# Four wide Strassen groups for the merge gates, and projections by tokens, in a hybrid encoder block

## The chip, the cores and the metric

The kernel runs on one core of one Trainium2 chip. The metric is device microseconds from the start to the end of one launch, as the median of three runs. TensorE (PE) multiplies, VectorE (DVE), ScalarE (ACT) and GpSimd (POOL) work on rows, and SyncE (SP) issues the transfers.

## The reference

One layer of a hybrid encoder, 512 tokens by 2048, in float32. A normed input is projected to 10752 columns; two attention branches, each gated by a SiLU, are projected to 2048 columns, merged by sigmoid gates, projected once more and added to the input:

```python
h = rmsnorm(x, norm_g[l])
proj = jnp.einsum('bsd,dc->bsc', h, w_in[l])
qa, ka, va, za, qb, kb, vb, zb, ga, gb = jnp.split(proj, SPLIT_POINTS, axis=-1)
...
ya = jnp.einsum('bsc,cd->bsd', oa * jax.nn.silu(za), w_out_a[l])
qb = axial_rope(rmsnorm(qb.reshape(B, S, N_HEADS_B, DH_B), q_norm_g[l]))
kb = axial_rope(rmsnorm(kb.reshape(B, S, N_KV_B, DH_B), k_norm_g[l]))
...
yb = jnp.einsum('bsc,cd->bsd', ob * jax.nn.silu(zb), w_out_b[l])
merged = jax.nn.sigmoid(ga) * ya + jax.nn.sigmoid(gb) * yb
x = x + jnp.einsum('bsd,de->bse', merged, w_o[l])
return rmsnorm(x, final_g)
```

Branch A is a differential attention of 8 heads, branch B a grouped one of 8 query and 2 key heads.

## The kernel before

Every product is made of three matmuls: both operands are split into a high part and a low rest (`hi_lo`: the high part is cast by ACT on line 111, the rest subtracted by VectorE on line 112), and high by high, low by high and high by low are summed in PSUM. The weights stream from memory into eight raw tiles; `split_w` takes three pairs of split tiles in turn, so the casts run up to three tiles ahead of TensorE.

The stages in order of time: the norm of x and a first group of plain columns (to 69.5 us); a narrow Strassen group (to 109.8); two wide Strassen groups for the other columns of q, k and v (`strassen_wide`, 111.3 to 263.7); twelve narrow Strassen groups by columns for the gates (`strassen`, 265.5 to 750.4), four for the SiLU gates z and then eight for the merge gates; the attention (750.4 to 1109.8), whose heads are interleaved with plain blocks of q and k and then with the projection `w_out_b` as filler (`fill`); the projection `w_out_a` with the merge (1109.8 to 1196.8); four narrow Strassen groups for `w_o` with the residual and the last norm.

A narrow group multiplies 512 tokens by 512 columns in seven products (a11, a12, s1, s2, s3, s4, a22) of 48 matmuls, 256 columns wide, on line 241: 336 matmuls. A wide group covers 512 tokens by 1024 columns with the same seven products of 48 matmuls, 512 wide, on line 322. A product of a narrow gate group takes two weight tiles of 128x1024, each cast once; VectorE also subtracts weight tiles (line 216) and adds products (line 642), and ACT applies the gate's function (line 643).

The order on each engine is that in which the code is recorded, moved by a scheduler's priorities; each engine then runs in order, and so does SP, whose transfers all pass through one queue. A waiting instruction keeps everything behind it on its engine waiting.

After each of the first ten gate groups `rope_b(n)` turns one head of branch B (n below 8 are query heads, 8 and 9 key heads): SP loads it (`cols`, line 595), ACT squares its four token blocks (line 600), GpSimd makes the reciprocal root (`rb`, lines 107 and 108), VectorE does two half-width multiplications, one full multiplication and an addition (lines 611 to 613), ACT scales key heads by `rb` (line 616), and SP stores it (line 617). The order of heads is `to_rope`. The attention's first heads load what was stored (line 673).

PSUM is eight banks. `new_banks` opens a pool of single banks or of pairs of banks; `share_banks` names the rings for accumulators (`acc`) and for the rest (`aux`), and `bank` takes the next of a ring. In the attention there are two `acc` and six `aux` banks. A head's `scores(i)` (branch A, lines 788 and 789) make four tiles of weights, `turn_p` transposes them on TensorE (line 732), `finish` multiplies with the values, and `norm` (branch A, lines 813 to 824) sums squares by two matmuls and applies the norm through ACT (816, 817, 820) and VectorE (from 821).

Of the kernel before, what the change touches and what calls it, by code (L numbers as in the profile page):

```python
# [17 lines left out]
P = 128  # L18
D = 2048
# [32 lines left out]
def hybrid_block_kernel(  # L52
# [16 lines left out]
    def new_banks(unit):  # L69
        ps_pools.close()  # L70
        banks["pool"] = unit, ps_pools.enter_context(
            tc.tile_pool(name="ps_" + unit, bufs=1, space=bass.MemoryType.PSUM))
# [120 lines left out]
    def strassen(w, c_left, c_right, act, natural, tmp, done, tail=None, before={}):  # L193
# [24 lines left out]
        def product(name, b, by_row=False, parts=None):  # L218
            if name in before:
                before[name]()  # L220
            ps = [acc_tile(256) for _ in range(2)] if by_row else acc_tile(2, 256)
# [5 lines left out]
            for n, (p, u) in enumerate(steps):  # L227
                if p not in parts:
                    parts[p] = split_w(b[p])
                hi, lo = parts[p]  # L230
# [138 lines left out]
    gg = dram.tile([2 * D, S], F32, name="gg")  # L369
    og = dram.tile([2 * BW, S], F32, name="og")  # L370
    yg = dram.tile([D, S], F32, name="yg")
# [59 lines left out]
    with tc.tile_pool(name="xs", bufs=1) as xs:  # L431
# [119 lines left out]
        with tc.tile_pool(name="wide", bufs=1) as wide:  # L551
            for n, blocks in enumerate(WIDE_BLOCKS):
                def kept(th, ch, v, blocks=blocks):
                    keep_cols(blocks[ch * 4:ch * 4 + 4], th * 2, 2, v)

                strassen_wide(w_in, column_pieces(blocks[:4]), column_pieces(blocks[4:]), xq, wide, kept, late=n == 0)
        slots[:] = slots[0:2] + slots[4:6] + slots[2:4] + slots[6:8]

        with tc.tile_pool(name="sp", bufs=6) as sp:
# [29 lines left out]
            def rope_b(n):  # L589
# [31 lines left out]
            to_rope = [0, 8, 1, 2, 3, 4, 5, 9, 6, 7]  # L621
# [15 lines left out]
            for c0, n, func, dst in ((O_ZA, BW, AF.Silu, zg[0:BW]), (O_ZB, BW, AF.Silu, zg[BW:]),  # L637
                                     (O_GA, D, AF.Sigmoid, gg[0:D]), (O_GB, D, AF.Sigmoid, gg[D:])):
                for g in range(0, n, S):
                    def gate(th, ch, ps, sb, g=g, func=func, dst=dst):  # L640
                        v = tmp()
                        nc.vector.tensor_tensor(out=v, in0=ps, in1=sb, op=ALU.add)
                        nc.scalar.activation(out=v, in_=v, func=func)
# [6 lines left out]
                    if to_rope:  # L650
                        rope_b(to_rope.pop(0))

    share_banks(acc=[4, 5], aux=[6, 7, 0, 1, 2, 3])
# [66 lines left out]
    class Head:  # L720
# [6 lines left out]
        def turn_p(self):  # L727
            self.pt = []
            for j in range(NT):
# [151 lines left out]
    def og_act(k):  # L881
        return tuple(v[:, k % 8, :] for v in ogq[k // 8])
# [24 lines left out]
    def fillers():  # L907
# [9 lines left out]
        for n in range(8):  # L917
            def yb_done(c, ps, n=n):
                j = c * 8 + n
                g = load_rows(gg, NK + j, "kq", 2)  # L920
                nc.vector.tensor_tensor(out=g, in0=ps, in1=g, op=ALU.mult)
                nc.sync.dma_start(out=yg[j * P:(j + 1) * P, :], in_=g)

            steps = stream_steps(w_out_b, [(n * P, P), (1024 + n * P, P)], 8, False, lambda k: og_act(8 + k), yb_done)
            for last in (12, 12, 16, 16):
# [15 lines left out]
    with tc.manual_schedule(engines={mybir.EngineType.PE}):  # L941
# [7 lines left out]
        for n, head in enumerate(heads):  # L949
            f = [int(c) for c in FILLS[n]]  # L950
            last = heads[n - 1] if n else None
            if n + 1 < len(heads):
                heads[n + 1].double()
            head.scores(0)
# [4 lines left out]
            head.scores(2)  # L959
            head.scores(3)  # L960
# [18 lines left out]
    share_banks(acc=list(banks["aux"] + banks["acc"]), aux=[])  # L979
# [7 lines left out]
    with tc.tile_pool(name="ya", bufs=1) as yp:  # L987
        def row(src, j, tag):
            g = yp.tile([P, S], F32, name="rows", tag=tag, bufs=2)
            nc.sync.dma_start(out=g, in_=src[j * P:(j + 1) * P, :])  # L990
            return g

        for n in range(4):
            mg = yp.tile([P, 4, S], F32, name="mg", tag="mg")

            def ya_done(c, ps, n=n, mg=mg):
                j = c // 2 * 8 + n * 2 + c % 2
                g = row(gg, j, "g")
                yb = row(yg, j, "yb")

                with tc.high_priority() if n == 3 else ExitStack():
                    nc.vector.tensor_tensor(out=g, in0=ps, in1=g, op=ALU.mult)
                    nc.vector.tensor_tensor(out=mg[:, c, :], in0=g, in1=yb, op=ALU.add)

            stream(w_out_a, [(n * 256, 256), (1024 + n * 256, 256)], 8, False, og_act, ya_done)
            b = slice(n * 2, n * 2 + 2)
            a11, a12, a21, a22 = (mg[:, k * 2:k * 2 + 2, t * 256:t * 256 + 256]
                                  for t, k in ((0, 0), (0, 1), (1, 0), (1, 1)))
# [3 lines left out]
            m_sums = {"a11": (a11, ()), "a12": (a12, ()), "s1": (s, (s, a21, a22, ALU.add)),  # L1012
                      "s2": (s, (s, s, a11, ALU.subtract)), "s3": (s3, (s3, a11, a21, ALU.subtract)),
                      "s4": (s, (s, a12, s, ALU.subtract)), "a22": (a22, ())}

            def put(name, b=b, m_sums=m_sums):
                src, first = m_sums[name]
# [188 lines left out]
```

## Time and profile before

| | us |
|---|---|
| median of three runs (lowest, highest) | 1368.19 (1367.49, 1370.12) |
| the profiled execution's own time | 1369.72 |
| its span | 1367.5 |
| TensorE busy in the span | 1337.8 |
| VectorE / ACT / GpSimd busy | 1086.4 / 709.5 / 166.9 |

The span is the time from the first to the last instruction of the profiled execution; the own time counts what lies around it too. An engine's busy time is an average over stages with different limits, so the stages are to be read one by one. A matmul's listed duration contains its pipeline, so the pace of matmuls is read from start to start. "Idle before" names what ended a wait.

### The profile page before, as it was taken

The page shows a single profiled execution, that of the slowest core. Times are in us where ns is not written, and L with a number is a line of the kernel's source. Part 1 is how long each engine was busy: PE and PEld are TensorE (multiplying, and loading weights), DVE is VectorE, ACT ScalarE, POOL GpSimd, SP SyncE. Part 2 cuts the span into 40 slices and gives each one's busy share as a digit, 9 for nine tenths or more (in the row PEclk, how much of TensorE's full clock was granted, in tenths as well). Part 3 has the DMA queues.
Part 4 walks back from the last instruction along what each step waited for, and adds up shares of the span by engine and source line. Part 5 has one row for each costly group of instructions (what it writes and reads, how often), then busy time and mean ns, then how long its engine had stood idle before and what let it go on. Part 6 is the DMA issues. An engine that isn't in the chain of part 4 may idle for free.

```text
span 1367.5 us, 22737 instructions
## 1 busy us (share of the span) xinstructions
PE 1337.8 (98%) x8905; PEld 1232.9 (90%) x8905; DVE 1086.4 (79%) x1339; ACT 709.5 (52%) x1119; POOL 166.9 (12%) x154
## 2 busy tenths in 40 slices
PE   6999999999999999999999999999899999999997
PEld 5998888899999999999999888888688888899997
DVE  5976977777888777888876487977899948799886
ACT  7643343344445444444444576666777743354444
POOL 1000000040000000000000411331321010004322
PEclk9999999999999999999999999999999999999999
DMA  8244663564444545444455684455665446473233
GB/s 292 78 140 138 188 197 95 171 197 147 131 139 126 161 154 162 128 136 130 126 154 169 209 247 120 143 155 156 198 187 158 147 147 213 141 252 118 93 94 124
DMA packets 198892, 214.11 MB, mean 157 GB/s; under 512 B 11760, under 2 KB 159488, under 8 KB 198144
## 3 DMA queue, kind: packets, MB, share of 16 engines
q1 hardware_dynamic: 198784, 212.65, 50.0%
q8 instruction: 70, 1.15, 0.4%
q14 instruction: 38, 0.31, 0.1%
HBM read 172.76 MB, written 35.65 MB: 152 GB/s over the span
## 4 chain that ended last, share of the span: by engine, by line
PE 88%; DVE 5%; ACT 2%; DMA 2%; issue 2%; SPq 1%; POOL 0%; DVEq 0%; POOLq 0%; ACTq 0%
PE acc L241 45%; PE acc L182 23%; PE acc L322 11%; PE aux L745 3%; DVE w_lo L112 2%; PE aux L732 2%; PE aux L858 1%; PE aux L788 1%; PE aux L789 1%; DVE w_raw L216 1%; DMA xt<-in_x_dram 1%; ACT w_hi L111 0%; PE aux L481 0%; DMA lam<-in_lambda_k_dram 0%; DMA rows<-og 0%
## 5 line engine op out<-in xcount | busy, mean ns | idle before, releaser
L111 ACT CAST w_hi<-w_raw 128x1024 fp32r<-128x1024 f32 x357 | 374.9, 1051 | 495.7 <-PE acc L241 308.2
L112 DVE TENSOR_TENSOR w_lo<-w_raw,w_hi 128x1024 fp32r<-128x1024 f32 x357 | 449.1, 1260 | 159.3 <-ACT w_hi L111 158.9
L216 DVE TENSOR_TENSOR w_raw<-w_raw 128x1024 f32<-128x1024 f32 x136 | 170.8, 1256 | 2.1
L241 PE MATMUL acc<-a2h,w_hi 128*128 128x256 f32 x384 | 108.7, 283 | 0.0
L241 PE MATMUL acc<-a2l,w_hi 128*128 128x256 f32 x384 | 108.7, 283 | 0.0
L241 PE MATMUL acc<-a2h,w_lo 128*128 128x256 f32 x384 | 108.7, 283 | 0.0
L241 PEld LDWEIGHTS acc<-a2h,w_hi 128*128 128x128 f32 x384 | 73.7, 192 | 0.0
L241 PEld LDWEIGHTS acc<-a2l,w_hi 128*128 128x128 f32 x384 | 73.7, 192 | 0.0
L241 PEld LDWEIGHTS acc<-a2h,w_lo 128*128 128x128 f32 x384 | 73.7, 192 | 0.0
L700 DVE TENSOR_REDUCE nmax<-aux 128x1 f32<-128x512 f32 x96 | 61.4, 679 | 3.0 <-PE aux L789 3.0
L182 PE MATMUL acc<-a1h,w_hi 128*128 128x512 f32 (+1 forms) x160 | 57.3, 363 | 0.2 <-ACT a1h L485 0.2
L182 PE MATMUL acc<-a1h,w_lo 128*128 128x512 f32 (+1 forms) x160 | 56.5, 358 | 0.0
L182 PE MATMUL acc<-a1l,w_hi 128*128 128x512 f32 (+1 forms) x160 | 56.3, 357 | 0.1
L241 PE MATMUL acc<-a1h,w_hi 128*128 128x256 f32 x192 | 54.4, 283 | 1.6 <-DVE wide_u L330 1.6
L182 PE MATMUL acc<-a2h,w_hi 128*128 128x512 f32 (+1 forms) x160 | 55.6, 350 | 0.0
L182 PE MATMUL acc<-a2l,w_hi 128*128 128x512 f32 (+1 forms) x160 | 55.5, 348 | 0.0
L182 PE MATMUL acc<-a2h,w_lo 128*128 128x512 f32 (+1 forms) x160 | 55.4, 347 | 0.0
L241 PE MATMUL acc<-s2h,w_lo 128*128 128x256 f32 x192 | 54.5, 284 | 0.6 <-DVE w_lo L112 0.6
L241 PE MATMUL acc<-s1h,w_lo 128*128 128x256 f32 x192 | 54.3, 283 | 0.0
L241 PE MATMUL acc<-s3l,w_hi 128*128 128x256 f32 x192 | 54.3, 283 | 0.0
L241 PE MATMUL acc<-s3h,w_lo 128*128 128x256 f32 x192 | 54.3, 283 | 0.0
L241 PE MATMUL acc<-a1l,w_hi 128*128 128x256 f32 x192 | 54.3, 283 | 0.0
(353 smaller groups left out, 4177.6 us busy)
## 6 DMA issues: line engine op xcount, KB each, us to landing
w_raw<-in_w_in_dram SPq DMA_DIRECT2D x144, 512.0 KB, 3.8
w_raw<-in_w_in_dram SPq DMA_DIRECT2D x64, 256.0 KB, 4.1
w_raw<-in_w_o_dram SPq DMA_DIRECT2D x32, 512.0 KB, 4.2
cols<-pv SPq DMA_DIRECT2D x36, 256.0 KB, 3.3
gg<-kept SPq DMA_DIRECT2D x32, 256.0 KB, 2.4
w_raw<-in_w_out_b_dram SPq DMA_DIRECT2D x32, 256.0 KB, 3.7
rows<-gg SPq DMA_DIRECT2D x32, 256.0 KB, 3.4
w_raw<-in_w_out_a_dram SPq DMA_DIRECT2D x32, 256.0 KB, 3.2
```

Of the source, the lines that this page charges most:

```text
L111: nc.scalar.copy(out=hi, in_=src)
L112: nc.vector.tensor_tensor(out=lo, in0=src, in1=hi.bitcast(F32), op=ALU.subtract)
L182: nc.tensor.matmul(out=acc[b][:, place], lhsT=l, rhs=r, start=first and kc == order[0] and k == 0 and i == 0, stop=last and kc == order[-1 ...
L216: nc.vector.tensor_tensor(out=d, in0=u, in1=v, op=ALU.subtract)
L241: nc.tensor.matmul(out=ps[u] if by_row else ps[:, u, :], lhsT=l, rhs=r, start=n % (2 if by_row else 4) == 0 and k == 0 and i == 0, stop=n ...
L322: nc.tensor.matmul(out=ps[:, u, :], lhsT=l[:, kk, sl], rhs=r[:, k, :], start=kk == 0 and i == 0, stop=kk == H - 1 and i == 2)
L700: nc.vector.tensor_reduce(out=nmax, in_=sps, axis=AX.X, op=ALU.max, negate=True)
L732: nc.tensor.transpose(out=tp[:, i * P:(i + 1) * P], in_=self.p[i][:, j * P:(j + 1) * P], identity=ident)
L745: nc.tensor.matmul(out=o, lhsT=l, rhs=r, start=j == 0 and i == 0, stop=j == NT - 1 and i == 2)
L788: nc.tensor.matmul(out=sp, lhsT=qs[:, sl], rhs=kh, start=True, stop=False)
L789: nc.tensor.matmul(out=sp, lhsT=qs[:, sl], rhs=kl, start=False, stop=True)
L858: nc.tensor.matmul(out=sp, lhsT=l, rhs=r, start=n == 0, stop=n == 2)
```

## The change

Eight narrow merge-gate groups become four wide ones, which now stand right behind the two wide groups of q, k and v, ahead of the SiLU gates; their result `gg` is kept by tokens (512 by 4096) and not by columns. Both output projections are made by tokens (four accumulators of 128 tokens by 512 columns). The merged rows are then turned for `w_o` by 64 transposes on TensorE (`merged_turned`), the last lot of them inside the first product of the next stage, through the new argument `amid` of `strassen`.

Because the gate groups that are left are four, the ten heads of `rope_b` are handed out three, three, two and two behind them; their multiplications and additions are GpSimd's. `new_banks` claims all places of a pool in a fixed order. When the filler of `w_out_b` begins, two `aux` banks go over to the accumulators; heads that run with under six `aux` banks (`few`) share out their filler in another way and transpose in two parts. A head's norm moves behind the next head's `turn_p`. `w_o` has four accumulators and four other banks instead of eight accumulators.

```diff
     def new_banks(unit):
...
+        n = {"bank": 1, "pair": 2}[unit]
+        for i in range(8 // n):
+            pool.tile([P, n, S], F32, name="place", tag=f"{unit}{i}")
+        banks["pool"] = unit, pool
...
+            for g in range(0, 2 * D, 2 * S):
+                def merge_gate(th, ch, v, g=g):
+                    nc.scalar.activation(out=v, in_=v, func=AF.Sigmoid)
+                    c = g + ch * S
+                    nc.sync.dma_start(
+                        out=gg[th * 256:th * 256 + 256, c:c + S].rearrange("(u p) n -> p u n", p=P), in_=v)
+
+                strassen_wide(w_in, [(O_GA + g, S)], [(O_GA + g + S, S)], xq, wide, merge_gate)
...
-                    tc.keep_in_program_order(nc.vector.tensor_tensor(out=d, in0=s, in1=m, op=ALU.mult))
-                nc.vector.tensor_tensor(out=v, in0=v, in1=tcb, op=ALU.mult)
-                nc.vector.tensor_tensor(out=v, in0=v, in1=t2, op=ALU.add)
+                    nc.gpsimd.tensor_tensor(out=d, in0=s, in1=m, op=ALU.mult)
+                nc.gpsimd.tensor_tensor(out=v, in0=v, in1=tcb, op=ALU.mult)
+                nc.gpsimd.tensor_tensor(out=v, in0=v, in1=t2, op=ALU.add)
...
-            to_rope = [0, 8, 1, 2, 3, 4, 5, 9, 6, 7]
+            to_rope = [(0, 8, 1), (2, 3, 4), (5, 9), (6, 7)]
...
-            for c0, n, func, dst in ((O_ZA, BW, AF.Silu, zg[0:BW]), (O_ZB, BW, AF.Silu, zg[BW:]),
-                                     (O_GA, D, AF.Sigmoid, gg[0:D]), (O_GB, D, AF.Sigmoid, gg[D:])):
-                for g in range(0, n, S):
+            for c0, dst in ((O_ZA, zg[0:BW]), (O_ZB, zg[BW:])):
+                for g in range(0, BW, S):
...
-                    if to_rope:
-                        rope_b(to_rope.pop(0))
+                    for n in to_rope.pop(0):
+                        rope_b(n)
...
+        ring = banks["aux"]
+        banks["acc"] += [ring.pop(0), ring.pop(0)]
+        for n in range(4):
+            def yb_done(t, ps, n=n):
...
+            steps = stream_steps(w_out_b, [(n * S, S)], 8, True, lambda k, t: og_act(8 + k, t), yb_done)
...
+            few = len(banks["aux"]) < 6
...
-            fill(f[1] - 1)
+            fill(f[1] - few)
+            if few:
+                head.turn_p((0, 1))
+                fill(1)
+                head.turn_p((2, 3))
+            else:
+                head.turn_p()
             if last:
                 last.norm()
-            fill(1)
-            head.turn_p()
-            fill(f[2])
+            fill(f[2] - few)
...
-    share_banks(acc=list(banks["aux"] + banks["acc"]), aux=[])
+    share_banks(acc=banks["acc"], aux=banks["aux"])
...
+        def merged_turned(n, rows):
+
+            qs = [[aux(2, 256) for _ in range(2)] for _ in range(2)]
+            for th in range(2):
+                for kh in range(2):
+                    for j in range(2):
+                        for u in range(2):
+                            nc.tensor.transpose(out=qs[th][kh][:, j, u * P:u * P + P],
+                                                in_=rows[th * 2 + u][:, kh * 256 + j * P:kh * 256 + j * P + P],
+                                                identity=ident)
...
+            steps = stream_steps(w_out_a, [(n * 256, 256), (1024 + n * 256, 256)], 8, True, og_act, ya_done)
+            for i, _ in enumerate(steps):
+                if i == 2 and n:
+                    put = merged_turned(n - 1, turned_rows[-1])
...
+        strassen(w_o, 0, 256, mq, True, y_tmp, o_first, before={k: (lambda k=k: put_last(k)) for k in names[1:]},
+                 amid={"a11": lambda: put_last("a11")})
```

How the instructions stand now is shown at three places. On ACT, at the start of the second gate group, before the change (heads 8; the casts from `w_hi_3418` on are the group's fourth tile and later, `bsq` is a head's squares, `kept` a gate):

```order
L643 ACTIVATE kept_3291<-kept_3291 128x512
L600 ACTIVATE bsq_3297,rb_94<-cols_3295 128x128 x4
L111 CAST w_hi_3418<-w_raw_3320 128x1024
L111 CAST w_hi_3449<-w_raw_3314 128x1024
L616 ACTIVATE cols_3295<-cols_3295,rb_94 128x128 x4
L256 COPY kept_3387<-acc_3330 128x512
L111 CAST w_hi_3477<-w_raw_3316 128x1024
```

The same place after it, where the group begins with head 0 and then has head 8:

```order
L659 ACTIVATE kept_4975<-kept_4975 128x512
L617 ACTIVATE bsq_4981,rb_94<-cols_4979 128x128 x4
L115 CAST w_hi_5132<-w_raw_5034 128x1024
L617 ACTIVATE bsq_4996,rb_94<-cols_4994 128x128 x4
L115 CAST w_hi_5163<-w_raw_5028 128x1024
L633 ACTIVATE cols_4994<-cols_4994,rb_94 128x128 x4
L263 COPY kept_5101<-acc_5044 128x512
L115 CAST w_hi_5191<-w_raw_5030 128x1024
L617 ACTIVATE bsq_5015,rb_94<-cols_5013 128x128 x4
```

The scaling of head 8 (line 616, now 633) keeps its place ahead of the copy and of the cast of product s1's second tile, and a second head's squares have come between.

On SP, about the third gate group, before the change (one store and one load of a head in the group):

```order
L645 DMA zg_82<-kept_3694 128x2x256
L645 DMA zg_82<-kept_3755 128x2x256
L617 DMA pv_86<-cols_3759 128x512
L595 DMA cols_4679<-pv_86 128x512
L645 DMA zg_82<-kept_3965 128x2x256
```

The same queue after it, with heads 2 (`cols_5473`), 3 (`cols_5488`) and 4 (`cols_5503`) in one group:

```order
L661 DMA zg_82<-kept_5408 128x2x256
L661 DMA zg_82<-kept_5469 128x2x256
L634 DMA pv_86<-cols_5473 128x512
L634 DMA pv_86<-cols_5488 128x512
L612 DMA cols_5503<-pv_86 128x512
L612 DMA cols_5963<-pv_86 128x512
L634 DMA pv_86<-cols_5503 128x512
```

The load of head 4 now stands behind the stores of two heads of its own group.

On TensorE, at a norm of a late head of branch A, before the change (filler products on both sides):

```order
L182 MATMUL acc_10990<-og1h_10030,w_lo_11129 128x512
L182 MATMUL acc_10990<-og1l_10031,w_hi_11128 128x512
L813 MATMUL aux_11164<-sqh_11039,ones_78 128x512
L814 MATMUL aux_11164<-sql_11040,ones_78 128x512
L182 MATMUL acc_11178<-og1h_10030,w_hi_11183 128x512
```

After it (`aux_9492` is the last turned weight tile, `aux_9522` the next head's first scores):

```order
L750 MATMUL aux_9492<-ident_66,p_9365 128x128
L831 MATMUL aux_9501<-sqh_9315,ones_78 128x512
L832 MATMUL aux_9501<-sql_9316,ones_78 128x512
L806 MATMUL aux_9522<-kh_9381,qs_9385 128x512
L807 MATMUL aux_9522<-kl_9382,qs_9385 128x512
L806 MATMUL aux_9529<-kh_9388,qs_9392 128x512
```

The norm's matmuls and the next scores now follow one another with no filler between.

## Rows read from the trace of the kernel before

**Rows 1.** The page: busy us, share of the span and instructions of each engine.

```profile
PE 1337.8 (98%) x8905; PEld 1232.9 (90%) x8905; DVE 1086.4 (79%) x1339; ACT 709.5 (52%) x1119; POOL 166.9 (12%) x154
```

**Rows 2.** Stretches: us, busy PE, PEld, DVE, ACT, POOL, clock, DMA share, GB/s.

```profile
263.50:268.00 4.50, 2.88 (x23) 2.52 (x22) 4.47 (x5) 1.04 (x1) 0.00 (x0) 1.00 0.32 93
122.30:252.86 130.56, 130.56 (x578) 108.11 (x576) 102.63 (x88) 52.48 (x51) 0.00 (x0) 1.00 0.51 157
427.88:750.44 322.56, 322.56 (x2691) 322.56 (x2689) 254.54 (x259) 152.03 (x213) 12.97 (x14) 1.00 0.46 143
967.00:973.00 6.00, 6.00 (x15) 4.64 (x16) 2.88 (x7) 4.46 (x9) 0.00 (x0) 0.50 0.88 258
```

**Rows 3.** TensorE's waits: for whom, us in total, times, longest.

```profile
PE acc L241 <- DVE wide_u L330: 1.6, 1, 1.6
PE acc L322 <- DVE xt L524: 1.4, 1, 1.4
```

**Rows 4.** TensorE in order of time, a lot of transposes: start, us, operation.

```profile
1020.80 1.91 PE L732 MATMUL aux<-ident,p 128*128 128x128 f32 x16
1022.46 0.47 PE L182 MATMUL acc<-og1h,w_hi 128*128 128x512 f32 x1
1022.78 0.39 PE L182 MATMUL acc<-og1h,w_lo 128*128 128x512 f32 x1
```

**Rows 5.** ACT in order of time, the gate group that begins at 347.24.

```profile
348.85 0.29 ACT L600 ACTIVATE bsq<-cols 128x128 f32<-128x128 f32 x1
...
354.03 1.28 ACT L616 ACTIVATE cols<-cols,rb 128x128 f32<-128x128 f32 x4
355.21 0.56 ACT L256 COPY kept<-acc 128x512 f32<-128x512 f32 x1
355.96 1.05 ACT L111 CAST w_hi<-w_raw 128x1024 fp32r<-128x1024 f32 x1 [0.18 <-PE acc L241]
```

**Rows 6.** GpSimd in order of time, that group and the attention's start.

```profile
350.63 0.52 POOL L107 TENSOR_SCALAR rb<-rb 128x4 f32<-128x4 f32 x1 [38.37 <-ACT bsq L600]
351.23 1.34 POOL L108 TENSOR_TENSOR rb<-rb,neg_half 128x4 f32<-128x4 f32 x1
...
768.04 1.29 POOL L689 TENSOR_TENSOR cols<-cols,other 128x512 f32<-128x512 f32 x1
769.30 2.27 POOL L688 TENSOR_TENSOR cols<-cols,ca 128x512 f32<-128x512 f32 x1
```

**Rows 7.** VectorE in order of time, that group, and at 1253.76 beside GpSimd.

```profile
351.02 0.68 DVE L612 TENSOR_TENSOR cols<-cols,tc_k 128x512 f32<-128x512 f32 x1
351.62 1.21 DVE L112 TENSOR_TENSOR w_lo<-w_raw,w_hi 128x1024 fp32r<-128x1024 f32 x1
...
1253.76 1.76 DVE L112 TENSOR_TENSOR w_lo<-w_raw,w_hi 128x1024 fp32r<-128x1024 f32 x1
```

**Rows 8.** GpSimd's groups by form: busy us, mean ns, idle before.

```profile
L689 POOL TENSOR_TENSOR cols<-cols,other 128x512 f32<-128x512 f32 x16 | 25.3, 1580 | 1.3
```

**Rows 9.** Transfers by line: count, KB each, median us from issue to landing.

```profile
cols<-pv SPq DMA_DIRECT2D x36, 256.0 KB, 3.3
```

**Rows 10.** SP's issues and TensorE's first turned head at the attention's start.

```profile
755.53 1.33 SPq L673 DMA_DIRECT2D cols<-pv  x3
...
766.79 1.04 PE L711 MATMUL aux<-ident,cols 128*128 128x128 f32 x8
```

**Rows 11.** TensorE in order of time, ahead of the dip of the clock.

```profile
964.20 0.50 PE L813 MATMUL aux<-sqh,ones 128*128 128x512 f32 x1 [1.23 <-ACT sqh L111]
...
966.96 0.79 PE L814 MATMUL aux<-sql,ones 128*128 128x512 f32 x1 [2.27 <-DVE sql L112]
```

**Rows 12.** ACT in order of time, a late head's norm.

```profile
1094.31 0.68 ACT L816 ACTIVATE y<-aux,eps_t 128x512 f32<-128x512 f32 x1
1095.02 0.63 ACT L817 ACTIVATE y<-y 128x512 f32<-128x512 f32 x1
```

More of the change, by code (lines that the diff above doesn't have):

```diff
@@ L191, in stream, with strassen @@
             pass
-    def strassen(w, c_left, c_right, act, natural, tmp, done, tail=None, before={}):
+    def strassen(w, c_left, c_right, act, natural, tmp, done, tail=None, before={}, amid={}):
         H = NK // 2
@@ L229, in product @@
                     parts[p] = split_w(b[p])
+                if late and n == 2:
+                    late()
                 hi, lo = parts[p]
@@ L725, in double, with turn_p @@
             pass
-        def turn_p(self):
-            self.pt = []
-            for j in range(NT):
+        def turn_p(self, part=range(NT)):
+            if 0 in part:
+                self.pt = []
+            for j in part:
                 tp = aux()
@@ L879, in og_tiles, with og_act @@
         ogq[half] = tuple(xa.tile([P, 8, S], F32R, name=f"og{half}{e}", tag=f"a{half + 1}{e}") for e in "hl")
[L881 to L882 removed]
+    def og_act(k, t=None):
+        return tuple(v[:, k % 8, :] if t is None else v[:, k % 8, t * P:t * P + P] for v in ogq[k // 8])
     def keep_og(k, v):
@@ L987, in hybrid_block_kernel, with row @@
     with tc.tile_pool(name="ya", bufs=1) as yp:
-        def row(src, j, tag):
-            g = yp.tile([P, S], F32, name="rows", tag=tag, bufs=2)
-            nc.sync.dma_start(out=g, in_=src[j * P:(j + 1) * P, :])
-            return g
[L993 to L1005, printed above, removed]
+        def row(src, t, c0, n, tag, bufs):
+            g = yp.tile([P, S], F32, name="rows", tag=tag, bufs=bufs)
+            for k in range(2):
+                c = c0 + k * 1024 + n * 256
+                nc.sync.dma_start(out=g[:, k * 256:k * 256 + 256], in_=src[t * P:(t + 1) * P, c:c + 256])
+            return g
@@ L1021, in put, with ya_done, put_last @@
                 hi_lo(mq[name][0][:, b, :], mq[name][1][:, b, :], src)
-            if n < 3:
-                for name in m_sums:
-                    put(name)
+            return put
+        names = ("a11", "a12", "s1", "s2", "s3", "s4", "a22")
+        turned_rows = []
+        for n in range(4):
+            rows = [None] * NT
+            def ya_done(t, ps, n=n, rows=rows):
+                rows[t] = g = row(gg, t, 0, n, "g", 6)
+                yb = row(yg, t, 0, n, "yb", 2)
+                with tc.high_priority() if n == 3 else ExitStack():
+                    nc.vector.tensor_tensor(out=g, in0=ps, in1=g, op=ALU.mult)
+                    nc.vector.tensor_tensor(out=g, in0=g, in1=yb, op=ALU.add)
+            steps = stream_steps(w_out_a, [(n * 256, 256), (1024 + n * 256, 256)], 8, True, og_act, ya_done)
+            for i, _ in enumerate(steps):
+                if i == 2 and n:
+                    put = merged_turned(n - 1, turned_rows[-1])
+                    for name in names:
+                        put(name)
+            turned_rows.append(rows)
+        last_put = []
+        def put_last(name):
+            if not last_put:
+                last_put.append(merged_turned(3, turned_rows[-1]))
+            last_put[0](name)
         xr = [xa.tile([P, 2, D], F32, name="xr" + e, tag="a1" + e) for e in "hl"]
```

49 lines of the change are left out of this document (24 added, 25 removed).

## Prediction

> **What bounds the kernel now.** I read the page's busy line first: TensorE is busy for 1337.8 us, 98% of the span, VectorE 79%, GpSimd 12% [rows 1]. Then the table of stretches: in the wide and in the narrow gate stage alike TensorE is busy in every microsecond, with VectorE at 79% beside it [rows 2]. So a microsecond less of matmuls is a microsecond less of time, and each new wait of TensorE adds its length. Last the list of TensorE's waits, where two stand at the changes of PSUM's layout, to pairs of banks and back [rows 3].
>
> **The change part by part.** The sum is made against the profiled execution's own 1369.7 us; the median, 1368.2, is 1.5 below it, and I take the 1.5 off at the end.
>
> Merge gates. Eight narrow groups, 427.88 to 750.44, took 322.56 us for 8 x 336 matmuls of 256 columns: 120.0 ns each [rows 2]. Twelve wide products, 122.30 to 252.86, took 130.56 us for 576 matmuls of 512 columns: 226.67 ns each [rows 2]. Four wide groups of 336 are 304.6 us: **-17.9**. VectorE is no fuller in the wide stretch (102.6 of 130.6) than in the narrow one (254.5 of 322.6), so I expect the wide rate to hold.
>
> *A rule against it.* The Trainium skill (TensorE: Matmul & The Clock Gate, Back-to-back issue gap) has a fixed cost of about 2.5 ns for a warm matmul beside its columns. By it two narrow ones would exceed one wide by only 2.5 ns, an estimate of 3.4 us over 1344 pairs, not 17.9. The rows show 2 x 120.0 - 226.67 = 13.3 ns [rows 2], and the measurement decides.
>
> Turned rows. 64 transposes are new on TensorE, in four lots of 16. A lot took 1.66 us from its first to the next matmul, and that one 0.32 until its follower instead of 0.23 [rows 4]: 4 x 1.75 = **+7.0**.
>
> Fixed places. The waits of 1.4 and 1.6 at the two changes of PSUM's layout came because a new layout's tile waited for the last user of old banks [rows 3]. Fixed places let the first tile take the banks idle longest: **-3.0**.
>
> Rotary steps to GpSimd. This is the large unknown. In the group that begins at T = 347.24, ACT begins the four squares at T+1.6, the four scalings of line 616 at T+6.8, a copy, and at T+8.7 the cast of product s1's second tile [rows 5], which TensorE needs at T+14.4 (two products of 48 and half of one). GpSimd does only rsqrt, from T+3.39: 0.52 and 1.34 [rows 6]; the two half-width multiplications, the full one (0.68) and the addition are VectorE's [rows 7]. Afterwards GpSimd does all of it, for two or three heads in a row, and ACT's scaling of the second head stands where it did, with the copy and the cast behind it. No row shows these forms on GpSimd. The nearest are its 128x512 operations: 1.29 alone, 2.27 at worst, 1.58 in the mean of line 689 [rows 6, 8]; I take half of that for the half-width ones. At 1.58 the first head is done at T+3.4+0.5+1.6+1.3+1.6 = 8.4, the second at T+8.4+1.6+0.5+1.6+1.3+1.6 = 15.0 (13.6 at 1.29, 18.5 at 2.27). Then scaling 1.28, copy 0.56, cast 1.05 [rows 5] and the low half on VectorE 1.21 [rows 7]: T+19.1, against T+14.6 when the first low half is read: **+4.5** (3.1 to 8.0). The fourth gate group has the same order (heads 5 and 9): **+4.5**.
>
> In the third group SP holds the third head's load behind the store of the second, which waits for GpSimd until T+15.0. Two issues of 0.4 (three took 1.33 [rows 10]), landing 3.3 [rows 9], squares 1.6 (from 348.85 to about when GpSimd starts), cast 1.05 and low half 1.21 give T+23.0 against T+17.5 for product s2, whose first cast stands behind those squares: **+5.5** (4.1 to 9.0).
>
> At the attention's start, stores of heads 6 and 7 stand on SP ahead of the tables and of the first head's loads, which were issued at T+5.1 (T = 750.44); TensorE turned them at T+16.3 [rows 10]. Now: T+15.0, five issues 2.0, landing 3.3 make T+20.3: **+4.0** (2.6 to 7.5). Together +18.5 (12.9 to 32.5).
>
> VectorE is relieved of four operations a head, which buys nothing: nobody waited for them.
>
> *The same by another rule.* The Trainium skill (SBUF, Who interferes with whom) says that a VectorE instruction with two SBUF inputs and a GpSimd one that reads SBUF lock each other out. The trace agrees in direction: VectorE's 128x1024 subtraction took 1.21 us alone and 1.76 beside GpSimd [rows 7].
>
> Clock. After idle times of 1.23 and 2.27 us [rows 11] the granted clock was 0.50, the level of 1.2 GHz, for 6.0 us, which is a loss of 3.0; right after the wait of 1.6 at 265.5 it was 1.00 [rows 2]. For four waits of 4 to 5 us I take 1.5 each: **+6** (0 to 10).
>
> Late heads. The attention's ring of PSUM banks shrinks from six to four once the output projection runs beside it. For three heads the norm's two matmuls then stand right before the next head's scores, whose fourth tile takes the norm's bank again. Behind the norm come ACT's 0.68 and two of 0.63 [rows 12] and one VectorE operation of 0.68 [rows 7], about 3.1 us with the first matmuls' tail, against 1.4 until the bank is wanted: 3 x 1.7 = **+5** (0 to 10).
>
> Norm behind the turned weights. The waits of 1.23 and 2.27 [rows 11] came from ACT's late cast; a later norm gives part of it back, but the head's last weights are late as well: **-3** (-6 to 0).
>
> Tail of the merge. The last rows are turned after VectorE's adds, with one product as cover: **+1.5** (0 to 3). Natural instead of turned projections keep count and form of their matmuls: 0. More, smaller loads of gate rows: 0, while each is issued well ahead; a late one would cost about a landing of 3.3 [rows 9].
>
> Sum: -17.9 + 7.0 - 3.0 + 18.5 + 6 + 5 - 3 + 1.5 = +14.1. That is 1383.8 for a profiled execution and about **1382** as a median.
>
> **The rivals.**
> A: GpSimd hides its work. If a 128x512 operation of the rotary steps takes under 0.7 us, the second head is done by T+10.5, and the scaling, copy, cast and low half behind it (4.1) still meet T+14.6. The waits and the clock's loss go: 1368.2 - 17.9 + 7 - 3 + 5 - 3 + 1.5 = 1358, faster. For it: no row shows this form on GpSimd. Against it: none of its 128x512 rows is under 1.28.
> B: even. GpSimd stays at its 1.29 (stalls 12.9), single waits leave the clock alone, as that of 1.6 did [rows 2, 3], and the norm gives back 5: 1368.2 - 17.9 + 7 - 3 + 12.9 + 5 - 5 + 1.5 = 1369.
> C: mutual delay. At 2.27 per operation, and VectorE at 1.76, the stalls are 32.5 and the clock's loss 10: 1400.
> D: no gain by width. If a wide matmul in the merge gates takes two narrow ones' 240 ns, with all else as forecast, 17.9 is lost: 1400. Against it stand the 226.67 ns of 576 in a row. The skill's rule on the gap (the Trainium skill, TensorE: Matmul & The Clock Gate, Back-to-back issue gap) would come near it, at 1396.
>
> **How the numbers follow.** Forecast 0.60 at 1382, its own range 1372 to 1394; A 0.18, B 0.13, C 0.07, D 0.02. The range 1360 to 1398 leaves out most of A, C and the forecast's far ends, two in ten. About 0.2%, 2.7 us, is what a measurement of this kernel tells from no change: faster 0.18, same 0.13, slower 0.69.
>
> **What would show it.** Right: in the second, third and fourth gate group TensorE idles 3 to 9 us once, before the second tile of s1 (third group: the first of s2), released by VectorE's low half, with ACT's scaling or squares waiting for GpSimd or a load, and a dip of the granted clock behind it; wide merge gates at 226.7 ns; waits of 1 to 2 us on line 806 in the last heads; no waits at the changes of PSUM's layout. Wrong: GpSimd's operations under 0.7 us, or gate groups of 40.3 us.

## The result, and the profile after

The changed kernel takes 1410.57 us (1409.93 to 1411.66) beside 1368.12 us of the kernel before, a ratio of 1.0309 (95% interval 1.0291 to 1.0326). The forecast had the direction and the first of the mechanisms, but 1382, with 1398 as the end of its range. The span grew from 1367.5 to 1408.2 us, by 40.7; the sum had 14.1.

The busy line answers [rows 1]: TensorE is busy for only 4.6 us more, in a span that is 40.7 us longer.

```profile
PE 1342.4 (95%) x7625; PEld 1180.6 (84%) x7625; DVE 1079.7 (77%) x1271; ACT 714.5 (51%) x1104; POOL 224.1 (16%) x194
```

The table of stretches of the changed kernel, one stage in a line (length; busy time of PE, PEld, DVE, ACT, POOL; granted clock; DMA share; GB/s), answers [rows 2]:

```profile
112.00:570.89 458.89, 457.23 (x2017) 378.43 (x2017) 358.11 (x307) 198.65 (x191) 0.00 (x0) 1.00 0.52 165
611.27:659.82 48.55, 43.36 (x338) 42.86 (x337) 35.08 (x30) 22.83 (x47) 23.20 (x18) 0.93 0.44 142
630.50:634.00 3.50, 2.98 (x12) 2.69 (x13) 3.47 (x4) 3.40 (x11) 1.73 (x2) 0.50 0.29 95
659.82:711.32 51.50, 43.56 (x338) 43.06 (x337) 35.41 (x30) 21.57 (x43) 24.11 (x18) 0.90 0.42 133
711.32:759.42 48.10, 42.89 (x338) 42.39 (x337) 30.01 (x28) 21.44 (x39) 14.21 (x12) 0.93 0.49 142
759.42:1143.27 383.85, 360.94 (x1690) 297.15 (x1689) 292.74 (x495) 249.51 (x487) 92.91 (x65) 0.97 0.52 159
1143.27:1235.85 92.58, 92.58 (x433) 77.12 (x432) 62.63 (x86) 32.00 (x44) 1.28 (x1) 1.00 0.55 175
1235.85:1408.20 172.35, 163.69 (x1361) 163.07 (x1359) 151.07 (x160) 81.99 (x134) 44.37 (x36) 0.99 0.39 132
```

In order: the six wide groups; the second gate group, and in it 3.5 us at half the clock; the third; the fourth; the attention; the merge; the rest. The same stretches of the kernel before are these (the four z groups, the attention, the merge, the rest):

```profile
265.51:427.88 162.37, 161.78 (x1345) 161.46 (x1345) 128.48 (x132) 74.92 (x104) 20.96 (x30) 1.00 0.50 153
750.44:1109.76 359.32, 354.81 (x1691) 293.71 (x1689) 289.02 (x498) 243.99 (x473) 81.74 (x55) 0.99 0.57 170
1109.76:1196.80 87.04, 87.04 (x386) 72.10 (x384) 62.77 (x84) 29.78 (x39) 2.15 (x1) 1.00 0.54 173
1196.80:1367.50 170.70, 161.75 (x1345) 161.32 (x1343) 150.38 (x160) 80.91 (x133) 44.37 (x36) 0.98 0.39 136
```

Where the 40.7 us lie, stage by stage:

| stage | before | after | difference |
|---|---|---|---|
| start, up to the first wide product | 111.33 | 112.00 | +0.7 |
| wide groups, and the merge gates wherever they stand | 154.18 + 322.56 | 458.89 | -17.9 |
| first z group (570.89 to 611.27 now) | 41.41 | 40.38 | -1.0 |
| z groups 2 to 4 | 120.96 | 148.15 | +27.2 |
| attention | 359.32 | 383.85 | +24.5 |
| projection w_out_a with the merge | 87.04 | 92.58 | +5.5 |
| w_o to the end | 170.70 | 172.35 | +1.7 |

TensorE's waits in the changed kernel, for whom, us in total, times, longest, answer [rows 3]:

```profile
PE acc L248 <- ACT w_hi L115: 16.4, 3, 7.0
...
PE aux L806 <- DVE pl L116: 6.5, 3, 4.2
PE aux L728 <- DMA vb<-pv: 6.5, 1, 6.5
PE aux L806 <- DVE rows L887: 2.9, 1, 2.9
PE aux L750 <- DVE p L713: 2.6, 2, 1.5
...
PE acc L248 <- DVE w_lo L116: 2.1, 4, 1.0
PE acc L248 <- DVE wide_u L337: 1.7, 1, 1.7
PE acc L329 <- DVE xt L531: 1.4, 1, 1.4
```

The first line is one long wait in each of the z groups 2 to 4; L728 is the attention's start; L806 and L750 are scores and turned weights of late heads; the last two lines are the layout changes of [rows 3], still there.

GpSimd in the second z group (it begins at T = 611.27), start and us, answers [rows 6]:

```profile
614.66 0.99 POOL L111 TENSOR_SCALAR rb<-rb 128x4 f32<-128x4 f32 x1 [16.16 <-ACT bsq L617]
615.73 2.20 POOL L629 TENSOR_TENSOR cols<-cols,tc_q 128x512 f32<-128x512 f32 x1
...
618.87 1.69 POOL L630 TENSOR_TENSOR cols<-cols,rope 128x512 f32<-128x512 f32 x1
620.64 3.28 POOL L628 TENSOR_TENSOR rope<-cols,ts_k 128x256 f32<-128x256 f32 x2
...
626.51 1.26 POOL L630 TENSOR_TENSOR cols<-cols,rope 128x512 f32<-128x512 f32 x1
```

ACT behind it, answering [rows 5]:

```profile
627.81 1.27 ACT L633 ACTIVATE cols<-cols,rb 128x128 f32<-128x128 f32 x4 [9.65 <-POOL cols L630]
628.99 0.56 ACT L263 COPY kept<-acc 128x512 f32<-128x512 f32 x1
629.46 1.04 ACT L115 CAST w_hi<-w_raw 128x1024 fp32r<-128x1024 f32 x1
```

And TensorE behind that:

```profile
625.55 0.28 PE L248 MATMUL acc<-s1h,w_lo 128*128 128x256 f32 x1
630.55 0.58 PE L248 MATMUL acc<-s1h,w_hi 128*128 128x256 f32 x1 [4.72 <-ACT w_hi L115]
```

This is the forecast chain row for row: the second head is done at 627.77, T+16.5 (forecast T+15.0), ACT's scaling waits 9.65 us for it with the cast behind it, and TensorE stops in the middle of s1: its last matmul before the wait began at T+14.3. The wait ends with ACT's cast; the low half from VectorE, which the forecast named as what would release TensorE, adds only 0.47 us more.

In the third group it is SP: the stores of two heads stand at the head of its queue, and only then the third head's load is issued, at 678.64; ACT waits for it.

```profile
669.14 9.38 SPq L634 DMA_DIRECT2D pv<-cols  x2
678.64 1.93 SPq L612 DMA_DIRECT2D cols<-pv  x2
```

```profile
681.53 0.31 ACT L617 ACTIVATE bsq<-cols 128x128 f32<-128x128 f32 x1 [11.94 <-DMA cols<-pv]
```

In the attention something stands that the forecast had not. VectorE, behind the last lot of turned weights of a late head (L943 multiplies the projection w_out_b by its gate rows):

```profile
1103.48 0.69 DVE L943 TENSOR_TENSOR rows<-acc,rows 128x512 f32<-128x512 f32 x1 [0.62 <-DMA rows<-gg]
1105.12 0.69 DVE L943 TENSOR_TENSOR rows<-acc,rows 128x512 f32<-128x512 f32 x1 [0.95 <-DMA rows<-gg]
1105.73 1.28 DVE L116 TENSOR_TENSOR pl<-aux,ph 128x512 fp32r<-128x512 f32 x2
```

The four accumulators of a piece end together, the gate rows have two buffers, and the third and fourth product wait (0.62 and 0.95) for rows whose load waits for a store. The low parts of the turned weights (`pl`) stand behind them in VectorE's queue, and TensorE waits for those 4.15 us:

```profile
1106.47 0.80 PE L806 MATMUL aux<-kh,qs 128*128 128x512 f32 x1 [4.15 <-DVE pl L116]
```

### The profile page after: what moved, and what is told of

Its sections match the earlier page's. It is cut to its first block, busy times and chain, and to the rows that moved or that the text cites. A ratio compares the mean times of both kernels' runs of the same rounds, so it can differ in the third digit from the quotient of the medians.

```text
span 1408.2 us, 20166 instructions
## 1 busy us (share of the span) xinstructions
PE 1342.4 (95%) x7625; PEld 1180.6 (84%) x7625; DVE 1079.7 (77%) x1271; ACT 714.5 (51%) x1104; POOL 224.1 (16%) x194
## 5 line engine op out<-in xcount | busy, mean ns | idle before, releaser
L317 DVE TENSOR_TENSOR w_raw<-w_raw 128x1024 f32<-128x1024 f32 x96 | 116.8, 1222 | 23.6 <-DMA w_raw<-in_w_in_dram 22.5
L220 DVE TENSOR_TENSOR w_raw<-w_raw 128x1024 f32<-128x1024 f32 x72 | 97.7, 1357 | 0.9
L329 PE MATMUL acc<-w_hi,a2h 128*128 128x512 f32 x192 | 74.7, 389 | 0.0
L329 PE MATMUL acc<-w_hi,a2l 128*128 128x512 f32 x192 | 74.7, 389 | 0.0
L329 PE MATMUL acc<-w_lo,a2h 128*128 128x512 f32 x192 | 74.7, 389 | 0.0
L186 PE MATMUL acc<-w_hi,og1h 128*128 128x512 f32 x128 | 51.3, 401 | 0.0
L186 PE MATMUL acc<-w_lo,og1h 128*128 128x512 f32 x128 | 50.7, 396 | 0.0
L186 PE MATMUL acc<-w_hi,og1l 128*128 128x512 f32 x128 | 50.5, 394 | 0.0
L186 PE MATMUL acc<-w_hi,og0h 128*128 128x512 f32 x128 | 50.1, 392 | 0.0
L186 PE MATMUL acc<-w_hi,og0l 128*128 128x512 f32 x128 | 49.9, 390 | 0.0
L186 PE MATMUL acc<-w_lo,og0h 128*128 128x512 f32 x128 | 49.8, 389 | 0.0
```

Of the source, the lines that this page charges most:

```text
L186: nc.tensor.matmul(out=acc[b][:, place], lhsT=l, rhs=r, start=first and kc == order[0] and k == 0 and i == 0, stop=last and kc == order[-1 ...
L220: nc.vector.tensor_tensor(out=d, in0=u, in1=v, op=ALU.subtract)
L317: nc.vector.tensor_tensor(out=d, in0=u, in1=v, op=ALU.subtract)
L329: nc.tensor.matmul(out=ps[:, u, :], lhsT=l[:, kk, sl], rhs=r[:, k, :], start=kk == 0 and i == 0, stop=kk == H - 1 and i == 2)
```

## The experiments

The theory after the result had two parts. First, the z groups and the attention's start wait through the order of ACT and SP for two heads in a row on GpSimd. Second, the attention's late heads wait because the output projection by tokens takes two of the six banks, and its outputs come four at a time. The rivals: too many heads in one group whatever the engine, GpSimd's work slowing VectorE, and the moved norm.

**e1: the rotary operations back on VectorE.**

```diff
-                    nc.gpsimd.tensor_tensor(out=d, in0=s, in1=m, op=ALU.mult)
-                nc.gpsimd.tensor_tensor(out=v, in0=v, in1=tcb, op=ALU.mult)
-                nc.gpsimd.tensor_tensor(out=v, in0=v, in1=t2, op=ALU.add)
+                    tc.keep_in_program_order(nc.vector.tensor_tensor(out=d, in0=s, in1=m, op=ALU.mult))
+                nc.vector.tensor_tensor(out=v, in0=v, in1=tcb, op=ALU.mult)
+                nc.vector.tensor_tensor(out=v, in0=v, in1=t2, op=ALU.add)
```

> The changed kernel with the four rotary operations back on VectorE, heads still handed out three, three, two, two. Theory (GpSimd's chain, then ACT's and SP's order behind it): the gate groups 2 to 4, which took 48.55, 51.50 and 48.10 us, go back to 40.3 to 42 us, and the 6.5 us wait at the attention's start shrinks below 1 us, so about 33 us less than 1410.6: 1375 to 1380 us. Rival (three heads in one group are too many for whichever engine): at least 10 us of the 27 us stay in these groups, 1390 us or more. In both the waits of the late heads stay, since nothing of them is touched.

Measured: 1381.2 us (1377.7 to 1384.7, two executions), ratio 1.0093 (1.0058 to 1.0127), just above what was expected. The four z groups and the attention, in the stretches of this kernel:

```profile
570.86:732.89 162.03, 161.85 (x1345) 161.45 (x1346) 135.96 (x150) 85.15 (x150) 39.01 (x40) 1.00 0.57 173
732.89:1110.75 377.86, 358.79 (x1691) 294.77 (x1689) 297.91 (x503) 249.22 (x487) 89.31 (x59) 0.99 0.53 162
```

The z groups are at 162.0 us, where they were before the change (162.4), at full clock: all of their 27.2 us belonged to the operations' engine, none to three heads in a group. At the attention's start the wait is 0.2 us. The attention as a whole fell by 6.0, less than that wait and the dip of the clock behind it took, since small waits came up elsewhere (1.07 us of a new one behind the first head's turned weights, 0.84 for the accumulator of a plain block). 18.5 us of the attention's excess remain.

**e2: the key heads first in their groups**, GpSimd as in the change.

```diff
-            to_rope = [(0, 8, 1), (2, 3, 4), (5, 9), (6, 7)]
+            to_rope = [(8, 0, 1), (2, 3, 4), (9, 5), (6, 7)]
```

> The changed kernel with the key heads first in their groups, (8, 0, 1) and (9, 5) in place of (0, 8, 1) and (5, 9); GpSimd does the same operations. Theory (ACT's scaling of a key head waits for the second head's end on GpSimd, with the cast of s1's second tile behind it): the scaling now waits for the first head only, about T+9.5 instead of T+16.5, so gate groups 2 and 4 go from 48.55 and 48.10 to 40.3 to 42 us and the whole to about 1395 us; group 3 stays at 51 us. Rival (GpSimd's reads slow VectorE so much that the low halves are late): the groups stay within 2 us of what they were, 1408 to 1412 us.

Measured: 1409.56 us, no gain. Groups 2 and 4 became shorter, 45.44 and 46.88 instead of 48.55 and 48.10, far from 40.3, and group 3 became longer by 2.4. ACT in the second group, which begins at 611.44:

```profile
620.37 1.29 ACT L633 ACTIVATE cols<-cols,rb 128x128 f32<-128x128 f32 x4 [4.67 <-POOL cols L630]
...
623.11 1.03 ACT L115 CAST w_hi<-w_raw 128x1024 fp32r<-128x1024 f32 x1
```

The scaling is early, at T+8.9, as expected, but it now stands ahead of the first cast of s1 too, which TensorE needs at T+11.5 and which starts at T+11.7. The reordering moved the wait to an earlier tile instead of taking it away, and the expectation, which left that cast where it was, was wrong in size. The rival is not without a part: in groups 2 to 4 TensorE now waits 7.5 us for low halves and 9.8 for casts, where the change had 1.9 and 16.4. This is a low half in the second group, made while GpSimd was at work; with GpSimd idle the same operation took 1.22 (at 658.92 in the change):

```profile
626.57 2.31 DVE L116 TENSOR_TENSOR w_lo<-w_raw,w_hi 128x1024 fp32r<-128x1024 f32 x1
```

The experiment does not separate the two theories. e4 does for one head in a group.

**e4: the kernel before with the rotary operations on GpSimd, one head for each group** (the diff of the change's three lines alone).

> The kernel before with the rotary operations on GpSimd, one head behind each of the first ten gate groups as it was. Theory (two heads in a row are what makes the chain too long): one head ends on GpSimd at about T+9, the scaling of a key head, the copy, the cast and the low half end at about T+13, before T+14.6, and each group stays at 40.3 us: 1368 us, within 2 us. Rival (GpSimd's work as such delays VectorE and with it TensorE): 1 us or more for each of ten groups, 1378 us or more.

Measured: 1371.8 us, ratio 1.0028 (1.0016 to 1.0041), so 3.5 us slower. The stretches are the second gate group, which has a key head, and the third, which has a query head:

```profile
346.96:388.84 41.88, 40.81 (x338) 40.40 (x337) 30.47 (x30) 19.98 (x31) 6.85 (x6) 1.00 0.46 139
388.84:429.16 40.32, 40.32 (x338) 40.32 (x337) 32.41 (x30) 18.89 (x27) 9.10 (x6) 1.00 0.47 144
```

Both groups with a key head take 1.56 us more, and each group behind a query head 40.32 as before. With one head in a group, GpSimd's work beside VectorE costs TensorE nothing by itself; what costs is ACT's scaling of a key head, which waits here as well, with a cast behind it:

```profile
355.89 1.28 ACT L616 ACTIVATE cols<-cols,rb 128x128 f32<-128x128 f32 x4 [4.68 <-POOL cols L613]
```

The rival falls for one head in a group, and the theory was a little too kind: even one key head lengthens its group by 1.6 us. For two or three heads in a row VectorE's slower low halves were not tried by themselves.

**e3: the kernel before with the fixed places alone** (the diff of `new_banks` above), **and e10: the same with the first wide product in another pair of banks.**

```diff
-        share_banks(acc=[2, 3, 0, 1])
+        share_banks(acc=[0, 1, 2, 3])
```

> The kernel before with the fixed places of PSUM's banks alone. The prediction had the two waits at the layout changes, 1.4 and 1.6 us, go: 1365 us. The changed kernel still has 1.35 and 1.66 us there, so the theory now is that fixed places change neither: waits of 1.4 and 1.6 us stay and the time stays at 1368 us.

> The kernel before with the fixed places of e3, and the first wide product in another pair of PSUM's banks (ring 0, 1, 2, 3 instead of 2, 3, 0, 1). If TensorE's wait at the change to pairs is for the bank that VectorE still reads, it changes with the pair (to nothing or to over 1.4 us); if a new layout waits for all users of the old one, it stays at 1.35 us. The time stays at 1368 us within 2 us either way.

Measured: 1368.75 us for e3, ratio 0.9999 (0.9988 to 1.0009), and 1371.07 for the one run of e10. The wait at the change to pairs is the same in both; this is e10's line:

```profile
PE acc L326 <- DVE xt L528: 1.4, 1, 1.4
```

The places change nothing. With another pair the wait is still 1.36 us (1.35 in e3), so in both pairs tried the first product waits for the last user of the old layout, whichever bank it takes itself. The wait at the change back to single banks (1.62 in e3 and in e10) was not tried with other banks, and why the allocation does so was not tried either.

**e6: four buffers for the gate rows of w_out_b**, all else as changed.

```diff
-                g = at.tile([P, S], F32, name="rows", tag="kq", bufs=2)
+                g = at.tile([P, S], F32, name="rows", tag=("kq", "yb")[t % 2], bufs=2)
```

> The changed kernel with four buffers instead of two for the gate rows that the projection w_out_b is multiplied by. Theory (four accumulators end together, two buffers make the third and fourth product wait for a store and a load, and VectorE's queue waits with them): VectorE's waits for these rows (0.4 to 1.4 each) go, TensorE's wait of 4.15 us in the last of the late heads falls to the 1.2 of the others, and with the clock 4 to 6 us are saved: about 1405. Rival (that wait comes from the bank ring of four alone): it stays at 4 us, 1410.

Measured: 1404.6 us (1403.5 to 1405.7), 6.0 less than the change. In the list of waits the 4.2 is gone; the three heads now wait alike. Another wait has grown meanwhile, the one for the product of the last head of branch B, from 2.9 to 4.4:

```profile
PE aux L806 <- DVE rows L887: 4.4, 1, 4.4
PE aux L806 <- DVE pl L116: 3.6, 3, 1.2
```

In the profiled executions the attention falls by 4.4 us, from 383.85 to 379.44. The rival falls: the 4 us wait came from the rows.

**e5: the norm ahead of the turned weights again**, directly, with no filler between.

```diff
             fill(f[1] - few)
+            if last:
+                last.norm()
...
-            if last:
-                last.norm()
             fill(f[2] - few)
```

> The changed kernel with each head's norm ahead of the next head's turned weights again, as in the kernel before; all else as changed. Theory (right behind the norm the next scores want its bank): in the late heads the waits for VectorE's reading of the norm's tile (0.5 each) and part of those for the low parts of the weights (1.2 each) go, 3 to 5 us less than 1410.6; the 4 us wait of the last of these heads, which VectorE's gate products cause, stays. Rival (the later norm gives TensorE cover elsewhere, as the prediction had it): the waits ahead of the last head of branch B grow by 3 us or more and the total does not fall.

Measured: 1419.28 us, 8.7 slower than the change; the attention is 394.0 us. My theory of the norm falls. Of the rival's two signs one holds, the total does not fall: the later norm is worth some 9 us in the changed kernel, against a norm with no filler between it and the turned weights. The kernel before had a filler there, and that form was not tried with the ring of four. The other sign does not hold: the waits ahead of the last head of branch B do not grow (2.6 in the change, 2.5 here). The waits for the low parts nearly double, and the early heads of branch B wait for the norm's tile, which they did not:

```profile
PE aux L806 <- DVE pl L116: 12.1, 5, 4.5
...
PE aux L876 <- DVE y L839: 3.5, 2, 2.3
```

**e7: e1, e5 and e6 together.**

> The changed kernel with three edits together: rotary operations on VectorE, norm ahead of the turned weights, four buffers for the gate rows. If the three causes are separate, the sum of theirs: 1381 less 4 and less 5, about 1372; if the late heads' waits share one cause, the ring of four banks, about 1378.

Measured: 1378.55 us (1377.3 to 1382.8), ratio 1.0077 (1.0057 to 1.0097), with an attention of 379.95 us, which fits a gain of the rows and a loss of the norm's place that nearly cancel. It is e1's time less 2.7, within the spread of both, and near the 1378 of one shared cause; by itself it tells nothing apart.

**e8: rotary operations on VectorE, and w_out_b by tokens in pieces of 256 columns with two accumulators**, so that six other banks stay throughout.

```diff
-        ring = banks["aux"]
-        banks["acc"] += [ring.pop(0), ring.pop(0)]
-        for n in range(4):
+        for n in range(8):
...
-            steps = stream_steps(w_out_b, [(n * S, S)], 8, True, lambda k, t: og_act(8 + k, t), yb_done)
-            for last in (10, 10, 12, 12, 14, 14, 16, 16):
+            steps = stream_steps(w_out_b, [(n * 256, 256)], 8, True, lambda k, t: og_act(8 + k, t), yb_done)
+            for last in (12, 12, 16, 16):
...
-    share_banks(acc=banks["acc"], aux=banks["aux"])
+    share_banks(acc=banks["acc"] + banks["aux"][:2], aux=banks["aux"][2:])
```

> The changed kernel with the rotary operations on VectorE, and with w_out_b by tokens in eight pieces of 256 columns and two accumulators, so that the attention keeps six other banks throughout and no head is run in the form for few banks. 384 matmuls of 256 columns at 120.0 ns instead of 192 at 226.67 cost 2.6 us more. Theory (the ring of four is what the late heads wait for): the attention falls from 377.9 us towards the 359.3 of the kernel before plus 2.6, and the whole to 1362 to 1366 us, below the kernel before. Rival (the later norm, or the order of fillers, is the cause): the attention stays above 370 us and the whole at 1375 or more.

Measured: 1369.76 us (1368.3 to 1374.2), ratio 1.0015 (1.0003 to 1.0027); the attention is 369.16 us:

```profile
732.84:1102.00 369.16, 358.34 (x2075) 313.92 (x2074) 296.97 (x506) 248.60 (x489) 89.21 (x59) 1.00 0.54 167
```

No wait on L806 is left in this kernel's list. The attention falls by 8.7 us against e1, although it does more: the projection is 384 matmuls of 512 columns, not the 192 of the expectation, and 768 of 256 at 120.0 ns cost 5.1 us more. So what e8 takes away cost some 13.8 us, 8.7 measured and 5.1 worked out from the paces of matmuls: the ring of four, the form of the heads for few banks, and four accumulators that end together. e8 does not separate these three. The time lies between theory and rival; 4.7 us of the attention's excess are left beside the 5.1.

**e9: e8 with the loop over heads as in the kernel before**, the norm between two fillers.

```diff
-            fill(f[1] - few)
-            if few:
-                head.turn_p((0, 1))
-                fill(1)
-                head.turn_p((2, 3))
-            else:
-                head.turn_p()
+            fill(f[1] - 1)
             if last:
                 last.norm()
-            fill(f[2] - few)
+            fill(1)
+            head.turn_p()
+            fill(f[2])
```

> The kernel of e8 (rotary operations on VectorE, w_out_b by tokens in pieces of 256 columns with two accumulators) with the loop over heads as in the kernel before: the norm between two fillers, ahead of the turned weights. What is left of the change is the wide merge gates, the turned rows, and projections by tokens. If the later norm is what the attention of e8 (369.2 us against 359.3) still waits for, mostly in small waits of 0.5 to 2.7 us, the attention falls to 362 to 364 us and the whole to 1361 to 1365 us, below the kernel before. If the order of rows and loads of the new projection is the cause, it stays within 2 us of e8, 1368 to 1371.

Measured: 1367.86 us (1364.2 to 1372.0), ratio 0.9996 (0.9986 to 1.0007): as fast as the kernel before, not faster. The attention is 368.06 us, 1.1 below e8. The norm's place isn't what the attention of e8 waits for, and the expectation of 1361 to 1365 was wrong. What is left of the excess over 359.32, some 3.6 us beside the 5.1, is in small waits in other places than before. The largest new one is of the projection, for an accumulator that VectorE has not yet multiplied by its gate rows:

```profile
1017.34 0.39 PE L186 MATMUL acc<-w_hi,og1h 128*128 128x256 f32 x1 [2.43 <-DVE rows L941]
```

VectorE had stood 3.81 us before, for a cast that ACT made only after 6.63 us of waiting for GpSimd's product of a head (line 842). Whether the rest has a common cause stays open. So the best version found equals the kernel before: the 17.9 us of the merge gates pay for 7.2 of turned rows and 8.7 of attention, and little is left.

## Why the prediction was wrong

**Merge gates: right.** -17.9 forecast, 154.18 + 322.56 to 458.89 is -17.9. 226.67 ns held over six wide groups. Against the fixed gap of the Trainium skill (TensorE: Matmul & The Clock Gate, Back-to-back issue gap) the row of the kernel was the better guide (13.3 ns between two narrow matmuls and a wide one, not 2.5), and rival D falls.

**Turned rows and tail: right.** +8.5 forecast in all, +5.5 and +1.7 measured, 7.2; three of the four lots lie in the first stage and the last in the second, and the tail's own wait did not come.

**Fixed places: wrong**, 3.0 us. That step took the waits for waits for a bank. e3 shows that fixed places change neither, and e10 that the first does not go with the bank that is taken.

**Rotary steps: right in mechanism and place, too small.** Each of the three groups stopped at the product that was named, behind the instruction that was named. Forecast 14.5 us of waits and 4.5 for the clock; the list has 16.4 for the casts and 1.9 for the low halves in these groups, 18.3, and of the 27.2 the other 8.9 are the clock. Two terms were mis-sized.

The first is GpSimd's chain. The sum gave each operation one price, from means. In the trace the same operation took two different times, by what VectorE did meanwhile; the rows show that the two go together, and no run changed VectorE's work alone. The two half-width operations of a query head took 3.28 us while VectorE subtracted weight tiles and 1.40 while VectorE stood waiting, both in the third group:

```profile
669.19 3.28 POOL L628 TENSOR_TENSOR rope<-cols,ts_q 128x256 f32<-128x256 f32 x2
...
681.58 1.40 POOL L628 TENSOR_TENSOR rope<-cols,ts_q 128x256 f32<-128x256 f32 x2 [3.41 <-DMA cols<-pv]
```

VectorE was slower in the same stretch: two subtractions took 3.88 us beside GpSimd and 2.48 with GpSimd idle.

```profile
668.00 3.88 DVE L220 TENSOR_TENSOR w_raw<-w_raw 128x1024 f32<-128x1024 f32 x2
...
684.20 1.75 DVE L116 TENSOR_TENSOR w_lo<-w_raw,w_hi 128x1024 fp32r<-128x1024 f32 x1 [8.13 <-ACT w_hi L115]
...
708.02 2.48 DVE L220 TENSOR_TENSOR w_raw<-w_raw 128x1024 f32<-128x1024 f32 x2
```

So half of a full operation, 0.79, was a fair price with VectorE waiting (0.70), and less than half of the price beside it (1.64). The full-width operations show the same two levels, 2.20 at 615.73 and 1.26 at 626.51 in the rows above; their means, 1.53 and 1.74, were close to the 1.58 of the sum and hid this. In the second group the half-width operations of the second head took 1.7 us more than forecast, and what followed them, with VectorE waiting, 1.2 less than forecast. The prediction had this effect for VectorE's operations, and for GpSimd's in rival C only, which got 0.07: measured waits of 18.3 and 6.5 at the attention's start lie between the forecast's 18.5 and C's 32.5. One of its rows was not what it was called: VectorE's 1.21 "alone" at 351.62 ran beside GpSimd's small 128x4 operation of 351.23 [rows 6, 7]. At 348.75, with GpSimd idle, the same operation took 1.22, so the figure stands.

The second is the clock's loss, taken as 1.5 a wait. It was 3.0 in the mean of these three, the full loss of the row that the term was made from, which I had halved without a reason.

**Attention's start: right place, 4.0 forecast, 6.5 measured**; e1 takes it away. Which of the chain's operations make up these 2.5 us was not followed.

**Late heads, norm and loads of gate rows: the step that failed most.** The sum had +5, -3 and 0 there, and +4.0 and +1.5 for the start, 7.5 for the whole attention; it was 24.5. Of these, 18.4 are more idle time of TensorE (22.9 against 4.5), where the sum had 6.0, and 6.1 are longer matmuls at the lower clock (354.81 to 360.94 busy, with nearly the same count, 1691 and 1690), where it had 1.5 for the start and nothing for the late heads.

The waits of L806 were forecast for the norm's bank alone, 1.7 a head; that wait came to 1.0 in all. Those that came first were for another tile of the same ring of four, the turned weights whose low part VectorE still has to make, 6.5 us, and for the product of the last head of branch B, 2.9. "More, smaller loads of gate rows: 0, while each is issued well ahead" is where the largest of them, 4.15 us, is from: the projection by tokens ends four accumulators at once, with two buffers behind them, and VectorE's queue stops (e6: 6.0 us). The ring of four, the form for few banks and the accumulators that end together cost about 13.8 us in all (e8 against e1); how much of that is the ring's alone was not tried. Of the waits ahead of the last head of branch B the norm's move took 0.9 at most, not 3 (2.6 on L750 now, 1.2 + 2.3 before). With six other banks the norm's place made 1.1 us of difference (e8 against e9); with four, a norm with no filler behind it cost 8.7 more (e5).

Of the 26.6 us between the sum and the result, 17.0 are the attention's, 8.2 the z groups', 3.0 the places'; the rest gives 1.6 back. The 7.5 against 24.5 decided that the time left its range: without those 17.0 it would have been 1393.6.

## What to carry to other kernels

When work moves to a slower engine, follow its result into every in-order queue that waits for it, ACT's and the transfers' alike: one wait there holds up whatever is queued behind, and the next stage's operands among it. When a product is laid out so that its accumulators end together, count buffers and banks for the burst, not for the mean. Price an operation by what runs beside it, not by its mean. A lost clock belongs to each wait of some microseconds, at the price that a row of such a wait shows and not at half of it; the price is not fixed even for equal waits, as the next section shows.

## What the runs showed of the hardware that was not expected

GpSimd and VectorE slowed each other in both directions. GpSimd's 128x256 operations took 0.70 us each while VectorE waited and 1.64 beside its subtractions of weight tiles; the two subtractions took 1.40 us longer than without GpSimd (3.88 and 2.48).

After a wait of 4.72 us at TensorE the granted clock was 0.50, the level of 1.2 GHz, for the 3.5 us of the shown stretch, while right after the two waits of 1.35 and 1.66 us it was 1.00. Nearly equal waits at the same place of the attention did not cost the same: in the 6.0 us behind the wait of 4.15 the mean granted clock was 0.58, and behind that of 4.32 us in e1 it was 0.72.

```profile
1106.40:1112.40 6.00, 5.93 (x16) 4.70 (x17) 5.17 (x11) 2.45 (x6) 1.28 (x1) 0.58 0.55 181
```

```profile
1074.60:1080.60 6.00, 5.95 (x19) 4.59 (x20) 5.15 (x10) 2.44 (x6) 1.29 (x1) 0.72 0.60 182
```
